# A hybrid decoder layer on one core: x is read and normalized early, the product behind the cross attention takes plain pairs first, and a simulated timeline sets the order

## The chip, the core and the metric

The kernel runs on one core of one Trainium2 chip, as one program. The metric is device time in microseconds (us) of that core from the start to the end of an execution; the times shown are medians of several executions. A core has a matmul engine (PE, with its weight loads as PEld), a vector engine (DVE), a scalar engine (ACT), a general engine (POOL) and a queue engine that issues transfers (SP). Each runs its own list of instructions in the listed order; an instruction waits until those it depends on, on whatever engine, have ended.

## The reference

One layer on 256 rows of 2048 fp32 numbers (one batch, D_FF 5632, 256 memory rows). Everything is fp32:

```
h = x
h = h + 0.5 * swiglu(rmsnorm(h, g_ffn1), w1_gate, w1_up, w1_down)     # silu(n@w_gate) * (n@w_up) @ w_down
z = rmsnorm(h, g_mix) @ w_in                                          # u, v | q | k, v
y_a = spatial_gating(u, v)        # gelu, rmsnorm of v, causal 128x128 mix of rows in 8 channel groups
y_b = window_attention_sinks(q, k, v, sinks)   # 16 heads of 64 on 2 kv heads, window 128, one sink logit a head
h = h + concat(rmsnorm(y_a), rmsnorm(y_b)) @ w_out
h = h + cross_attention(rmsnorm(h, g_x), rmsnorm(mem, g_mem), w_xq, w_xkv, w_xo)   # 4 heads of 512
h = h + 0.5 * swiglu(rmsnorm(h, g_ffn2), w2_gate, w2_up, w2_down)
out = rmsnorm(h, g_final)
```

with rmsnorm(x, g) = x * rsqrt(mean(x^2) + 1e-5) * g. The window attention is a masked softmax over 256 keys (128 in the first block) plus the sink; the cross attention is a plain softmax over the 256 memory rows.

## The kernel before

**Tiling.** The 256 rows are two blocks (TB = 2) of 128; h stays on chip for the whole program as two blocks of 128 x 2048. A product of fp32 numbers is made of three fast matmuls: each operand is split into a rounded high part and the rest as a low part, and high x high, low x high and high x low are added up in one PSUM bank. One such matmul is 128x128 by 128x512. The left operand is the activation, transposed, in *pairs* (two slices of 128 along the contraction by two row blocks, 128x4x128); the right operand is a *chunk* of weights, 128x4x512 fp32 (1 MB): two slices of the contraction by two column blocks. Multiplying a pair with a chunk is 24 matmuls (kinds N, plain, and C, with two sums) or 21 (kind S, a seven-product scheme with sums of the activation and of the weights, as in Strassen's). A *Unit* (L297) is a row of pairs and chunks that add up in the same banks, the four blocks of 256 rows by 1024 columns: products P, Q and R with numbers; names in `late` take their bank from the pool of transposes (trp, 4 banks), the others from the accumulation pool (acc, 4 banks).

**Weights.** `load` (L268 to L296) brings a chunk from HBM by SP into `raw` (3 buffers; L290 in four pieces for the first chunk, L293 for whole ones, L275 for kind S), makes the high part `wh` by a cast on ACT (L137) and the low part `wl` by a subtraction on DVE (L138), 2 buffers each; kind S adds sums on DVE and their split `t`, `th`, `tl` (1 buffer each). `push` (L341) loads a chunk and then issues the matmuls of the chunk before it (L324), so loads run one chunk ahead in the text.

**Stages.** f1 (gate/up units 0 to 10, then four down units), n2, kv, q, v, u with the spatial mix, window attention with the products mv of the memory values, mk, wo, n3, xq and the four heads of the cross attention, the product xo behind it, n4, f2 (as f1), the final norm with the stores. Names in the trace carry the stage's letters: `f1gP` is bank P of a gate/up unit of f1, `n1s` a scaled row tile of norm n1, `mvwh` the high part of an mv chunk.

**The opening.** Gate/up unit 0 (`plain_gu_unit`, L496) is plain: its pairs n0 come from xT, a transposed copy of x in HBM (L233), scaled by the gain only, and the rows are scaled by 1/rms in the silu (L451). `prep1` (L605) is called ahead of each of its 8 chunks: it loads xT for two pairs at each even chunk; at chunks 2 to 5 it loads a quarter of x (L615) and takes its squares; at chunk 6 it makes the 1/rms, and at chunks 6 and 7 it scales the rows (`n1s`, L624, on ACT), transposes them on PE (L208) and splits them into the pairs n1 of units 1 to 10, whose kinds are CCSCSCSC.

**Norms.** `next_norm` gives `on_block`, called as each 128x512 block of h is done: squares on ACT, and once the first half is done a preliminary 1/rms, by which `scaled` (L565, tile `n4s` at L568 for n4) scales the row blocks for the transposes of the pairs.

**Window attention (L744 to L809).** Two row blocks by two halves of the heads, each half in groups of scores that fill one bank: scores (`sc`, L760, PE), scaling with the mask (`scs`, L769, DVE), maximum (L773) and three small steps (to `nmx`, L778) on DVE, exponentials (L780, ACT, one for each head of the group), four transposes (`pT`, L788, PE), their copy (`pTs`, L792, DVE), and the product with v (`wop`, L796, PE). The text has it ahead of the two mv units, whose four banks are evacuated by ACT (L817) into tiles `mv` of the pool m4. The scheduler mixes both.

**Cross attention.** Per head: transposes of xq, scores, softmax (`pr`, L922), transposes of the probabilities (`xpT`, L927), product with mv, and two pairs `xo` of kind KINDS_O (NSNSNSNN). `added_unit` (L426) then multiplies them with the chunks of w_xo in two units; at the last S pair `early` adds what the sums give to h, at the last pair `late` adds the four blocks and calls `on_block`.

**The end.** `on_final` (L971) takes squares and multiplies each block of h by the final gain (`hg`, L975); the 1/rms of each row block (L116, L120, L122) then scales the eight blocks (DVE at L987, ACT at L985), and SP stores them (L988).

**What sets the order.** The text names no order between engines. A scheduler (the tile framework) takes all instructions with their dependences and buffer lifetimes and writes each engine's list: it places an instruction once it counts as ready, by priorities in the order of the text. Pool sizes (s2 7 tiles of 128x512, m4 12 tiles of 128x1024) bound how far ahead anything may be placed.

Of the kernel before, what the change touches and what calls it, by code (L numbers as in the profile page):

```python
# [14 lines left out]
P = 128  # L15
# [15 lines left out]
def layer_kernel(  # L31
# [265 lines left out]
    class Unit:  # L297


        def __init__(self, s, kinds):  # L300
            self.s = s
            self.kinds = kinds
# [6 lines left out]
            self.mixed = "S" in kinds  # L309
# [4 lines left out]
        def multiply(self, p, b):  # L314
            for name, *terms in PRODUCTS[p.kind]:
                if name not in self.banks:
                    late = ("P1", "Q6", "Q7") + (("R",) if self.mixed else ())
                    pool, tag = (trp, "tr") if name in late else (acc, "acc")
                    self.banks[name] = pool.tile([P, 512], F32, tag=tag, name=nm(self.s + name))
# [60 lines left out]
    KINDS_O = "NSNSNSNN"  # L380

# [44 lines left out]
    def added_unit(s, w, cb, pairs, on_block, kinds=KINDS_O):  # L426
        u = Unit(s, kinds)
        early, late = adds(s, 1.0, 2 * cb, on_block)
        last = len(kinds) - 1
        for i in range(len(kinds)):  # L430
            push(
                u, i, w[i, cb], lambda i=i: pairs[i],
                lambda i=i: early(u) if i == kinds.rindex("S") else late(u) if i == last else None,
# [105 lines left out]
    def next_norm(s, gcol, kinds="NNNNNNNN"):  # L539
# [25 lines left out]
        def scaled(j):  # L565
            r = [s2(s + "s") for _ in range(TB)]
            for tb in range(TB):
                nc.scalar.activation(  # L568
                    r[tb], h[:, tb, j * 512:(j + 1) * 512], AF.Copy, scale=st["est"][:, tb:tb + 1]
                )  # L570
            make(j, lambda tb, c: r[tb][:, c - j * 512:c - j * 512 + P])
# [33 lines left out]
    def prep1(i):  # L605
# [6 lines left out]
        if 2 <= i < 6:  # L612
            j = i - 2
            hj = h[:, :, j * 512:(j + 1) * 512]
            nc.sync.dma_start(hj, x[:, j * 512:(j + 1) * 512].rearrange("(b p) d -> p b d", p=P))  # L615
            for tb in range(TB):
                square_into(parts1[:, tb, j:j + 1], hj[:, tb, :], 512)
        if i == 6:
            rs1.append(rstd_of(parts1, NG, D))
        if i >= 6:  # L620
            for j in (2 * (i - 6), 2 * (i - 6) + 1):
                r = [s2("n1s") for _ in range(TB)]
                for tb in range(TB):
                    nc.scalar.activation(  # L624
                        r[tb], h[:, tb, j * 512:(j + 1) * 512], AF.Copy, scale=rs1[0][:, tb:tb + 1]
                    )
                for q in range(2):
                    n1[2 * j + q] = pair_from_rows(
                        "n1", KINDS[2 * j + q],
# [430 lines left out]
```

## Time and profile before

| what | value |
|---|---|
| median of 3 runs | 2149.03 us (2147.45 to 2151.48) |
| the profiled execution: its own time | 2150.37 us |
| its span, first to last instruction | 2147.0 us |
| mean granted clock of PE | 0.991 |
| busy: PE / PEld / DVE / ACT / POOL | 98% / 80% / 76% / 52% / 1% |
| DMA | 402.14 MB, 187 GB/s over the span |

The page gives for each engine its busy time and number of instructions; the span in 40 slices, where each digit is a tenth of busy time; and the chain of work that ended last, followed back from the end. A group's row reads: line, engine, operation, result <- operands, shapes, count, busy time and mean, idle time before it, and the work that ended that idle time. A row of the timeline is start, duration, engine, line, operation, and in brackets how long the engine idled ahead of it and what for. A busy PE is one with a matmul in its pipeline; a 128x512 matmul that takes 0.39 from start to end lets the next start after about 0.227 us (24 of a chunk follow one another in some 5.4).

### The profile page before, as it was taken

Reading aid. Unit: us, or ns where it says so; the run is one execution under the profiler, and the core shown is the slowest. Engines: PE = TensorE matmul, PEld = TensorE weight load, DVE = VectorE, ACT = ScalarE, POOL = GpSimd, SP = SyncE. Lnnn points to the kernel's source line nnn. Section 1 sums busy time; section 2 is a strip of 40 time slices with the busy share of each in tenths; the row PEclk is TensorE's granted clock in tenths of the full one; section 3 lists DMA queues with packets and bytes.
Section 4 is the critical chain, followed back from the end, with each engine's and each line's share of the span. In section 5 each row is a group of like instructions: output and inputs, shape, how many; then the busy total and the mean of one; then the engine's idle time right before and its main releaser. Section 6 shows DMA issues by size and latency. Waiting matters only on the chain.

```text
span 2147.0 us, 23708 instructions
## 1 busy us (share of the span) xinstructions
PE 2097.3 (98%) x9529; PEld 1717.3 (80%) x9529; DVE 1626.8 (76%) x1540; ACT 1114.9 (52%) x1105; POOL 17.7 (1%) x35
## 2 busy tenths in 40 slices
PE   9799999999999999999999998999999999999997
PEld 7688888888888888878877887787888888878876
DVE  5688888888787745564568666898888888887876
ACT  7555554554554555444455454665555555555443
POOL 0000000000000010000000000000000000000000
PEclk9899999999999999999999999999999999999999
DMA  7355555555555576534545543455555555555553
GB/s 295 134 199 192 199 197 196 196 196 196 196 182 210 187 242 214 177 111 147 177 163 191 192 143 116 157 196 196 198 194 201 199 208 189 195 187 196 194 202 131
DMA packets 61805, 402.14 MB, mean 187 GB/s; under 512 B 6768, under 2 KB 10880, under 8 KB 14464
## 3 DMA queue, kind: packets, MB, share of 16 engines
q1 hardware_dynamic: 60448, 396.44, 51.4%
q0 software_dynamic: 1248, 4.20, 0.7%
q8 instruction: 74, 1.21, 0.2%
q14 instruction: 35, 0.29, 0.0%
HBM read 398.52 MB, written 2.10 MB: 187 GB/s over the span
## 4 chain that ended last, share of the span: by engine, by line
PE 90%; DVE 4%; ACT 3%; issue 1%; DMA 0%; POOL 0%; SPq 0%; POOLq 0%; DVEq 0%; ACTq 0%
PE f2gQ L324 15%; PE f1gQ L324 15%; PE f1dQ L324 6%; PE f2dQ L324 6%; PE f2gP L324 5%; PE f1gP L324 5%; PE f1dP L324 3%; PE f2dP L324 3%; PE f1dR L324 2%; PE mvQ L324 2%; PE f2dR L324 2%; PE mkQ L324 2%; PE xqQ L324 2%; PE woQ L324 2%; PE mvP L324 1%
## 5 line engine op out<-in xcount | busy, mean ns | idle before, releaser
L138 DVE TENSOR_TENSOR f1gwl<-f1gw,f1gwh 128x2048 fp32r<-128x2048 f32 (+1 forms) x91 | 184.2, 2042 | 40.6 <-ACT f1gwh L137 40.5
L137 ACT CAST f1gwh<-f1gw 128x2048 fp32r<-128x2048 f32 (+1 forms) x91 | 156.0, 1715 | 91.0 <-PE f1gQ L324 66.5
L137 ACT CAST f2gwh<-f2gw 128x1536 fp32r<-128x1536 f32 (+1 forms) x88 | 153.6, 1751 | 70.2 <-PE f2gQ L324 41.5
L138 DVE TENSOR_TENSOR f2gwl<-f2gw,f2gwh 128x1536 fp32r<-128x1536 f32 (+1 forms) x88 | 182.1, 2087 | 8.5 <-ACT f2gwh L137 8.1
L137 ACT CAST f2dwh<-f2dw 128x2048 fp32r<-128x2048 f32 (+1 forms) x44 | 79.9, 1815 | 104.1 <-PE f2dQ L324 86.2
L324 PE MATMUL f2gQ<-f2gwh,n4fh 128*128 128x512 f32 x341 | 133.0, 390 | 0.0
L324 PE MATMUL f2gQ<-f2gwh,n4fl 128*128 128x512 f32 x341 | 132.9, 390 | 0.0
L324 PE MATMUL f2gQ<-f2gwl,n4fh 128*128 128x512 f32 x341 | 132.6, 390 | 0.0
L324 PE MATMUL f1gQ<-f1gwh,n1fh 128*128 128x512 f32 x330 | 130.3, 395 | 0.0
L137 ACT CAST f1dwh<-f1dw 128x2048 fp32r<-128x2048 f32 (+1 forms) x44 | 79.9, 1815 | 95.9 <-PE f1dQ L324 80.6
L324 PE MATMUL f1gQ<-f1gwh,n1fl 128*128 128x512 f32 x330 | 128.9, 391 | 0.0
L324 PE MATMUL f1gQ<-f1gwl,n1fh 128*128 128x512 f32 x330 | 128.9, 391 | 0.0
L138 DVE TENSOR_TENSOR f1dwl<-f1dw,f1dwh 128x2048 fp32r<-128x2048 f32 (+1 forms) x44 | 95.3, 2169 | 37.6 <-ACT f1dwh L137 37.4
L138 DVE TENSOR_TENSOR f2dwl<-f2dw,f2dwh 128x2048 fp32r<-128x2048 f32 (+1 forms) x44 | 95.3, 2169 | 37.3 <-ACT f2dwh L137 37.2
L138 DVE TENSOR_TENSOR f2gtl<-f2gt,f2gth 128x2048 fp32r<-128x2048 f32 x33 | 75.6, 2292 | 53.9 <-ACT f2gth L137 51.8
L137 ACT CAST f2gth<-f2gt 128x2048 fp32r<-128x2048 f32 x33 | 63.1, 1911 | 95.0 <-DVE f2gt L284 95.0
L138 DVE TENSOR_TENSOR f1gtl<-f1gt,f1gth 128x2048 fp32r<-128x2048 f32 x30 | 68.8, 2292 | 45.3 <-ACT f1gth L137 45.3
L137 ACT CAST f1gth<-f1gt 128x2048 fp32r<-128x2048 f32 x30 | 57.4, 1913 | 67.8 <-DVE f1gt L284 65.3
L324 PEld LDWEIGHTS f2gQ<-f2gwh,n4fh 128*128 128x128 f32 x341 | 64.0, 188 | 13.4
L324 PEld LDWEIGHTS f2gQ<-f2gwh,n4fl 128*128 128x128 f32 x341 | 64.0, 188 | 13.3
L324 PEld LDWEIGHTS f2gQ<-f2gwl,n4fh 128*128 128x128 f32 x341 | 64.0, 188 | 13.3
L324 PEld LDWEIGHTS f1gQ<-f1gwl,n1fh 128*128 128x128 f32 x330 | 62.3, 189 | 13.3
(616 smaller groups left out, 5823.2 us busy)
## 6 DMA issues: line engine op xcount, KB each, us to landing
f2gw<-in_w_gu SPq DMA_DIRECT2D x88, 1024.0 KB, 4.8
f1gw<-in_w_gu SPq DMA_DIRECT2D x87, 1024.0 KB, 4.9
f1dw<-in_w_down SPq DMA_DIRECT2D x44, 1024.0 KB, 4.8
f2dw<-in_w_down SPq DMA_DIRECT2D x44, 1024.0 KB, 4.8
mvw<-in_w_xkv SPq DMA_DIRECT2D x16, 1024.0 KB, 4.8
mkw<-in_w_xkv SPq DMA_DIRECT2D x16, 1024.0 KB, 4.8
wow<-in_w_out SPq DMA_DIRECT2D x16, 1024.0 KB, 4.8
xqw<-in_w_xq SPq DMA_DIRECT2D x16, 1024.0 KB, 4.8
```

The source lines that it names most:

```text
L137: nc.scalar.copy(hi, src)
L138: nc.vector.tensor_tensor(lo, src, hi.bitcast(F32), ALU.subtract)
L324: nc.tensor.matmul(self.banks[name], x, y, start=name not in self.begun, stop=self.left[name] == 0,)
```

## The change

It does four things. **prep1**: x is loaded in four quarters at chunks 1 and 2, with the squares, the 1/rms is made at chunk 3, and each of chunks 4 to 7 scales one quarter, into one tile of pool m4 (128x1024) where two tiles of s2 stood, and makes two pairs of n1. **scaled** of `next_norm` uses one m4 tile in the same way. **The cross attention's product** takes pairs of kinds KINDS_X = NNNNSNSN, two S pairs where there were three, and names the products with a bank in the pool of transposes (P1, Q5, Q6, Q7, where R was and Q5 was not). **The scheduler** is told to go by a simulated timeline, in which each instruction has an estimated duration, when it chooses what to place next on an engine.

```diff
--- before.py
+++ after.py
@@ -297,8 +297,9 @@
     class Unit:
 
 
-        def __init__(self, s, kinds):
+        def __init__(self, s, kinds, late=("P1", "Q6", "Q7", "R")):
             self.s = s
+            self.late = late if "S" in kinds else ()
             self.kinds = kinds
             self.left = {}
             for kind in kinds:
@@ -306,7 +307,6 @@
                     self.left[name] = self.left.get(name, 0) + 3 * len(terms)
             self.begun = set()
             self.banks = {}
-            self.mixed = "S" in kinds
 
         def __getitem__(self, name):
             return self.banks[name]
@@ -314,8 +314,7 @@
         def multiply(self, p, b):
             for name, *terms in PRODUCTS[p.kind]:
                 if name not in self.banks:
-                    late = ("P1", "Q6", "Q7") + (("R",) if self.mixed else ())
-                    pool, tag = (trp, "tr") if name in late else (acc, "acc")
+                    pool, tag = (trp, "tr") if name in self.late else (acc, "acc")
                     self.banks[name] = pool.tile([P, 512], F32, tag=tag, name=nm(self.s + name))
                 for an, bn in terms:
                     (ah, al), (bh, bl) = p[an], b[bn]
@@ -378,6 +377,7 @@
 
     KINDS = "CCSCSCSC"
     KINDS_O = "NSNSNSNN"
+    KINDS_X = "NNNNSNSN"
 
     KINDS_D = "NNNNSNNN" + "NSNSNSN" + "NSNNNNN"
 
@@ -423,14 +423,14 @@
 
         return early, late
 
-    def added_unit(s, w, cb, pairs, on_block, kinds=KINDS_O):
-        u = Unit(s, kinds)
-        early, late = adds(s, 1.0, 2 * cb, on_block)
+    def added_unit(s, w, cb, pairs, on_block, kinds=KINDS_O, late=("P1", "Q6", "Q7", "R")):
+        u = Unit(s, kinds, late)
+        early, end = adds(s, 1.0, 2 * cb, on_block)
         last = len(kinds) - 1
         for i in range(len(kinds)):
             push(
                 u, i, w[i, cb], lambda i=i: pairs[i],
-                lambda i=i: early(u) if i == kinds.rindex("S") else late(u) if i == last else None,
+                lambda i=i: early(u) if i == kinds.rindex("S") else end(u) if i == last else None,
             )
 
     def ffn(s, get, rs, wgu, wd, on_block, first=None):
@@ -563,12 +563,12 @@
                 scaled(j)
 
         def scaled(j):
-            r = [s2(s + "s") for _ in range(TB)]
+            r = m4(s + "s").rearrange("p (b c) -> p b c", b=TB)
             for tb in range(TB):
                 nc.scalar.activation(
-                    r[tb], h[:, tb, j * 512:(j + 1) * 512], AF.Copy, scale=st["est"][:, tb:tb + 1]
+                    r[:, tb], h[:, tb, j * 512:(j + 1) * 512], AF.Copy, scale=st["est"][:, tb:tb + 1]
                 )
-            make(j, lambda tb, c: r[tb][:, c - j * 512:c - j * 512 + P])
+            make(j, lambda tb, c: r[:, tb, c - j * 512:c - j * 512 + P])
 
         def make(j, src):
             for i in (2 * j, 2 * j + 1):
@@ -609,27 +609,27 @@
             ]
             for q in range(2):
                 n0.append(pair_from_dram("n0", xT, i + q, G_FFN1, [t[:, q] for t in quad]))
-        if 2 <= i < 6:
-            j = i - 2
-            hj = h[:, :, j * 512:(j + 1) * 512]
-            nc.sync.dma_start(hj, x[:, j * 512:(j + 1) * 512].rearrange("(b p) d -> p b d", p=P))
+        if i in (1, 2):
+            for j in (2 * i - 2, 2 * i - 1):
+                hj = h[:, :, j * 512:(j + 1) * 512]
+                nc.sync.dma_start(hj, x[:, j * 512:(j + 1) * 512].rearrange("(b p) d -> p b d", p=P))
+                for tb in range(TB):
+                    square_into(parts1[:, tb, j:j + 1], hj[:, tb, :], 512)
+        if i == 3:
+            rs1.append(rstd_of(parts1, NG, D))
+        if i >= 4:
+            j = i - 4
+            r = m4("n1s").rearrange("p (b c) -> p b c", b=TB)
             for tb in range(TB):
-                square_into(parts1[:, tb, j:j + 1], hj[:, tb, :], 512)
-        if i == 6:
-            rs1.append(rstd_of(parts1, NG, D))
-        if i >= 6:
-            for j in (2 * (i - 6), 2 * (i - 6) + 1):
-                r = [s2("n1s") for _ in range(TB)]
-                for tb in range(TB):
-                    nc.scalar.activation(
-                        r[tb], h[:, tb, j * 512:(j + 1) * 512], AF.Copy, scale=rs1[0][:, tb:tb + 1]
-                    )
-                for q in range(2):
-                    n1[2 * j + q] = pair_from_rows(
-                        "n1", KINDS[2 * j + q],
-                        lambda tb, k: r[tb][:, (2 * q + k) * P:(2 * q + k + 1) * P],
-                        G_FFN1 + 4 * j + 2 * q,
-                    )
+                nc.scalar.activation(
+                    r[:, tb], h[:, tb, j * 512:(j + 1) * 512], AF.Copy, scale=rs1[0][:, tb:tb + 1]
+                )
+            for q in range(2):
+                n1[2 * j + q] = pair_from_rows(
+                    "n1", KINDS[2 * j + q],
+                    lambda tb, k: r[:, tb, (2 * q + k) * P:(2 * q + k + 1) * P],
+                    G_FFN1 + 4 * j + 2 * q,
+                )
 
     n2, on2, rs2_ = next_norm("n2", G_MIX)
     ffn(
@@ -941,7 +941,7 @@
                           for b in range(2) for m, p in ((vh, ph), (vh, pl), (vl, ph))]
                 products(pv[:, i, :], passes)
             i = 2 * hd + half
-            kind = KINDS_O[i]
+            kind = KINDS_X[i]
             xo.append(Pair("xo", kind))
             if kind == "N":
                 split(xo[i].base[0].rearrange("p k t -> p (k t)"),
@@ -956,7 +956,7 @@
 
     n4, on4, rs4_ = next_norm("n4", G_FFN2, KINDS)
     for cb in range(2):
-        added_unit("xo", w_xo, cb, xo, on4)
+        added_unit("xo", w_xo, cb, xo, on4, KINDS_X, ("P1", "Q5", "Q6", "Q7"))
     flush()
 
 
@@ -1053,7 +1053,7 @@
         for k, v in arrays.items()
     ]
     args.append(nc.dram_tensor("out", (T, D), F32, kind="ExternalOutput").ap())
-    with tile.TileContext(nc) as tc:
+    with tile.TileContext(nc, schedule_with_timeline_sim=True) as tc:
         layer_kernel(tc, *args)
     r = run_bass_kernel_spmd(nc, [arrays], core_ids=[0])
     return r.results[0]["out"].reshape(1, T, D)
```

The changed file is a line shorter from L310 on: its L323 is L324 of before, and so on.

The lists change in nearly every stage. Three places follow. First SP's list, from the first transfer of weights on (`f1gw`; `n0r` are pieces of xT, `h` quarters of x, numbers count tiles). Before:

```order
L290 DMA f1gw_129<-in_w_gu 128x512 x4
L293 DMA f1gw_144<-in_w_gu 128x2048
L233 DMA n0r_180<-in_xT 128x2x256
L233 DMA n0r_186<-in_xT 128x2x256
L615 DMA h<-in_x 128x2x512
L293 DMA f1gw_197<-in_w_gu 128x2048
L615 DMA h<-in_x 128x2x512
L293 DMA f1gw_232<-in_w_gu 128x2048
L233 DMA n0r_264<-in_xT 128x2x256
L233 DMA n0r_270<-in_xT 128x2x256
```

With the change:

```order
L290 DMA f1gw_129<-in_w_gu 128x512 x4
L615 DMA h<-in_x 128x2x512 x2
L293 DMA f1gw_154<-in_w_gu 128x2048
L615 DMA h<-in_x 128x2x512 x2
L293 DMA f1gw_212<-in_w_gu 128x2048
L293 DMA f1gw_248<-in_w_gu 128x2048
L233 DMA n0r_190<-in_xT 128x2x256
L233 DMA n0r_196<-in_xT 128x2x256
L233 DMA n0r_280<-in_xT 128x2x256
L233 DMA n0r_286<-in_xT 128x2x256
```

The four quarters of x stand in pairs around the second chunk, and the xT pieces of chunks 2 and 4 behind the fourth.

Next PE's list in the window attention, from the last matmuls of mv's first unit (`mvQ`) to the first of its second (`mvP`). Before:

```order
L324 MATMUL mvQ_1179_6706<-mvwh_6864,mTfh_6275 128x512
L788 MATMUL pT_6551<-ident,scs_6541 128x128 x2
L760 MATMUL sc_6569<-kT_5383,qT_5661 128x256
L788 MATMUL pT_6551<-ident,scs_6541 128x128 x2
L760 MATMUL sc_6569<-kT_5383,qT_5661 128x256
L324 MATMUL mvQ_1179_6706<-mvwh_6864,mTfl_6276 128x512
L324 MATMUL mvQ_1179_6706<-mvwl_6865,mTfh_6275 128x512
L796 MATMUL wop_6463<-vv_5376,pTs_6556 128x64
L796 MATMUL wop_6463<-vv_5381,pTs_6556 128x64
```

Two more products `wop` follow, then `mvP` of the second unit. With the change, its first rows:

```order
L323 MATMUL mvQ_1175_6702<-mvwl_6861,mTfh_6271 128x512
L796 MATMUL wop_6396<-vv_5372,pTs_6421 128x64 x4
L760 MATMUL sc_6427<-kT_5379,qT_5657 128x128 x4
L788 MATMUL pT_6444<-ident,scs_6432 128x128
L760 MATMUL sc_6462<-kT_5379,qT_5636 128x256 x2
L788 MATMUL pT_6444<-ident,scs_6432 128x128 x3
L796 MATMUL wop_6396<-vv_5372,pTs_6449 128x64 x4
L788 MATMUL pT_6475<-ident,scs_6465 128x128 x4
L796 MATMUL wop_6459<-vv_5372,pTs_6480 128x64
L796 MATMUL wop_6459<-vv_5377,pTs_6480 128x64
```

Between the first unit's last matmul and the second's first there are 62 attention instructions now, and no other; before, each group of the attention had matmuls of mv beside it up to here.

On ACT, the evacuation of the first bank of mv's first unit (L817) stands, before:

```order
L780 ACTIVATE scs_6436,den_6401<-scs_6436,nmx_6442 128x128 x4
L137 CAST mvwh_6834<-mvw_6833 128x2048
L780 ACTIVATE scs_6469,den_6464<-scs_6469,nmx_6475 128x256 x2
L137 CAST mvwh_6864<-mvw_6863 128x2048
L780 ACTIVATE scs_6493,den_6464<-scs_6493,nmx_6499 128x256 x2
L137 CAST mvwh_6922<-mvw_6921 128x2048
L780 ACTIVATE scs_6517,den_6464<-scs_6517,nmx_6523 128x256 x2
L802 ACTIVATE esk_6465<-esk_6465 128x8
L780 ACTIVATE scs_6541,den_6464<-scs_6541,nmx_6547 128x256 x2
L137 CAST mvwh_6928<-mvw_6927 128x2048
L817 ACTIVATE mv_6669<-mvP_1176_6685,rs_6333 128x512
```

and with the change:

```order
L780 ACTIVATE scs_6404,den_6397<-scs_6404,nmx_6410 128x128 x4
L137 CAST mvwh_6918<-mvw_6917 128x2048
L137 CAST mvwh_6924<-mvw_6923 128x2048
L802 ACTIVATE esk_6398<-esk_6398 128x8
L780 ACTIVATE scs_6432,den_6397<-scs_6432,nmx_6438 128x128 x4
L780 ACTIVATE scs_6465,den_6460<-scs_6465,nmx_6471 128x256 x2
L780 ACTIVATE scs_6489,den_6460<-scs_6489,nmx_6495 128x256 x2
L780 ACTIVATE scs_6513,den_6460<-scs_6513,nmx_6519 128x256 x2
L802 ACTIVATE esk_6461<-esk_6461 128x8
L780 ACTIVATE scs_6537,den_6460<-scs_6537,nmx_6543 128x256 x2
L780 ACTIVATE scs_6568,den_6563<-scs_6568,nmx_6574 128x256 x2
L817 ACTIVATE mv_6665<-mvP_1172_6681,rs_6329 128x512
```

The casts of mv's weights stood between the exponentials and now stand ahead of them; in both lists the evacuation stands behind the exponentials shown.

Last DVE's list at the end of the program, from the addition of the first block of the last down unit to the first scaled output. Before:

```order
L391 SCALAR_TENSOR_TENSOR h<-f2dP_2578_14849,h 128x512
L975 TENSOR_TENSOR hg_15067<-h,gf_10228 128x512
L391 SCALAR_TENSOR_TENSOR h<-f2dQ_2579_14856,h 128x512
L975 TENSOR_TENSOR hg_15072<-h,gf_10228 128x512
L391 SCALAR_TENSOR_TENSOR h<-f2dR_14863,h 128x512
L116 TENSOR_REDUCE ss_15084<-partsf_10230 128x1
L120 TENSOR_SCALAR ms_15086<-ss_15084 128x1
L987 TENSOR_SCALAR hg_14818<-hg_14818,rs_15088 128x512
```

With the change:

```order
L391 SCALAR_TENSOR_TENSOR h<-f2dP_2560_14818,h 128x512
L975 TENSOR_TENSOR hg_15036<-h,gf_10197 128x512
L391 SCALAR_TENSOR_TENSOR h<-f2dQ_2561_14825,h 128x512
L391 SCALAR_TENSOR_TENSOR h<-f2dR_14832,h 128x512
L975 TENSOR_TENSOR hg_15041<-h,gf_10197 128x512
L391 SCALAR_TENSOR_TENSOR h<-f2dQ_2563_14839,h 128x512
L116 TENSOR_REDUCE ss_15053<-partsf_10199 128x1
L975 TENSOR_TENSOR hg_15046<-h,gf_10197 128x512
L120 TENSOR_SCALAR ms_15055<-ss_15053 128x1
L987 TENSOR_SCALAR hg_14787<-hg_14787,rs_15057 128x512
```

The first scaled block stood behind three additions and two products with the gain; it stands now behind four and three.

In all, PE has 9432 instructions where it had 9426, DVE 1530 where it had 1542, ACT 1000 where it had 1007; those of SP and POOL that move data are as many as before.

## Prediction

> **What bounds the kernel now.** I read the page's busy shares and its chain of waits first, then busy time by stage, then what the matmul engine (PE) waited for. The page:
>
> ```profile
> PE 2097.3 (98%) x9529; PEld 1717.3 (80%) x9529; DVE 1626.8 (76%) x1540; ACT 1114.9 (52%) x1105; POOL 17.7 (1%) x35
> ...
> PE 90%; DVE 4%; ACT 3%; issue 1%; DMA 0%; POOL 0%; SPq 0%; POOLq 0%; DVEq 0%; ACTq 0%
> ```
>
> PE is busy for 2097.3 of 2147.0 us and carries 90% of the chain. An order of instructions can win only the 49.7 us in which PE is idle and what it loses at a lower clock, and it can lose as much as it likes. Where those microseconds lie, by stage (span; busy us of PE, PEld, DVE, ACT, POOL; granted clock; DMA share; GB/s):
>
> ```profile
> 54.00:107.00 53.00, 40.37 (x171) 32.43 (x170) 36.50 (x41) 29.01 (x37) 0.00 (x0) 0.84 0.36 133
> 107.00:805.00 698.00, 695.82 (x3166) 574.73 (x3165) 557.76 (x482) 362.05 (x304) 7.24 (x12) 1.00 0.55 199
> 912.00:966.00 54.00, 52.45 (x252) 39.95 (x252) 32.47 (x55) 22.66 (x48) 0.00 (x0) 0.97 0.32 113
> 1288.00:1342.00 54.00, 46.22 (x242) 38.90 (x241) 32.50 (x42) 24.05 (x37) 1.12 (x2) 0.94 0.32 116
> 1342.00:1396.00 54.00, 50.31 (x219) 40.04 (x217) 44.56 (x47) 34.24 (x42) 0.71 (x1) 0.97 0.43 156
> 1396.00:2093.00 697.00, 694.79 (x3088) 567.66 (x3089) 591.71 (x515) 368.21 (x291) 0.69 (x1) 1.00 0.55 197
> 2093.00:2147.00 54.00, 42.11 (x186) 34.53 (x184) 35.40 (x42) 21.66 (x28) 1.10 (x2) 0.93 0.37 132
> ```
>
> The two long feed-forward stretches idle 2.2 us each in some 700: nothing is to be had there. Four places hold nearly all: the end of gate/up unit 0 (12.6 us idle), the window attention (1.55), the cross attention with its product (7.8 and 3.7), the tail (11.9). What PE waited for there (us in total, times, longest):
>
> ```profile
> PE n L208 <- ACT n1s L624: 9.1, 3, 5.2
> PE xpT L927 <- DVE pr L922: 4.5, 2, 2.8
> PE f1gP L324 <- ACT f1sg L451: 3.6, 1, 3.6
> PE n L208 <- ACT n4s L568: 2.5, 1, 2.5
> ...
> PE mvP L324 <- ACT mv L817: 1.6, 1, 1.6
> ```
>
> **The opening: a gain.** Early x means that the 32 transposes of n1, with their scaling and splits, move from the end of unit 0 to chunks 2 to 6 of it, under its matmuls. Rows for the prices:
>
> ```profile
> 9.00:12.00 3.00, 3.00 (x8) 2.34 (x7) 1.17 (x2) 0.72 (x2) 0.00 (x0) 1.00 0.99 387
> ...
> 11.90 1.90 ACT L137 CAST f1gwh<-f1gw 128x2048 fp32r<-128x2048 f32 x1 [1.95 <-DMA f1gw<-in_w_gu]
> 13.71 1.70 ACT L131 ACTIVATE n0h<-n0r,sm 128x256 fp32r<-128x256 f32 x4
> ...
> 52.18 2.29 DVE L138 TENSOR_TENSOR f1gwl<-f1gw,f1gwh 128x2048 fp32r<-128x2048 f32 x1 [2.05 <-ACT f1gwh L137]
> ...
> 69.79 1.28 ACT L451 ACT_TABLE_LOAD   x1
> 71.08 0.69 ACT L451 ACTIVATE f1sg<-f1gP,rs 128x512 f32<-128x512 f32 x1
> ...
> 71.82 0.79 PE L324 MATMUL f1gP<-f1gwh,n1fh 128*128 128x512 f32 x1 [3.57 <-ACT f1sg L451]
> ...
> 86.62 0.39 PE L324 MATMUL f1gP<-f1gwh,n1fh 128*128 128x512 f32 x1
> ```
>
> First what it costs. One megabyte of x now stands ahead of weight chunk 1, at 387 GB/s 2.7 us, so its cast starts at 14.6 and not at 11.90 and ends at 16.5, when chunk 0 has been done for 0.8 us; its low part comes 0.4 late. Chunk 2 needs xT's second pieces, which SP now issues behind chunks 2 and 3, and on ACT the cast of chunk 3, on DVE its low part, stand ahead of their splits. Chunk 1 ends at about 22.3 and frees the buffer; cast 1.9 and one split 0.42 make 24.65 (a wait of 2.35), the low part 2.2 makes 26.85 (1.3 more). These 4.85 us are lost ahead of chunk 3. From there nothing waits by my walk: five chunks of 24 matmuls at 0.227 and 32 transposes at about 0.115 end unit 0 at 62.4. Unit 1 still needs bank P, emptied by the first silu: after the last cast (59.3), seven n1 pieces (3.2), the table load (1.28) and the silu (0.69) it is 64.5, and the cast of its second chunk ends at 66.4. 42 matmuls and 8 transposes later, unit 1's chunk 2 starts at 76.9, where the row has 86.62: 9.7 less. The clock may fall in the 2 us wait; half of a 1.6 us price leaves **8.9** (5 with waits that I missed; 17 if none of the waits occur and unit 1 starts at once).
>
> **Steady units, down products, n2, kv, q, v, u, mk, wo: nothing.** The new order sends eight matmuls of the next chunk's high part before its low part. I walked one f1 unit and the starts and ends of the stages: casts (1.9) and low parts (2.2) are ready before PE asks, as the two rows with 2.2 us idle say of before. At the start of f2 I find about **1.0** more waiting (cast of its second chunk behind the last xo chunk). The price if this cover is gone is a rival.
>
> **Window attention: a loss, the largest term.** Rows of one group of heads in before (score, mask and maximum on DVE, two exponentials on ACT, transposes, copy, product):
>
> ```profile
> 951.70 0.69 DVE L792 COPY pTs<-pT 128x512 f32<-128x512 f32 x1
> 952.32 0.69 DVE L769 SCALAR_TENSOR_TENSOR scs<-sc,band 128x512 f32<-128x512 f32 x1
> 953.05 0.69 DVE L773 TENSOR_REDUCE mx<-scs 128x2 f32<-128x512 f32 x1
> ...
> 954.04 0.16 DVE L778 TENSOR_SCALAR nmx<-mx 128x2 f32<-128x2 f32 x1
> ...
> 954.30 0.51 ACT L780 ACTIVATE scs<-scs,nmx 128x256 f32<-128x256 f32 x1
> 954.81 0.49 ACT L780 ACTIVATE scs<-scs,nmx 128x256 f32<-128x256 f32 x1
> ...
> 939.33 1.13 PE L760 MATMUL sc<-kT,qT 64*128 64x256 f32 x4
> ...
> 951.22 0.44 PE L788 MATMUL pT<-ident,scs 128*128 128x128 f32 x2
> ...
> 958.74 1.00 PE L796 MATMUL wop<-vv,pTs 128*128 128x64 f32 x8
> ...
> 960.55 0.68 ACT L817 ACTIVATE mv<-mvP,rs 128x512 f32<-128x512 f32 x1
> ...
> 962.00:964.00 2.00, 2.00 (x7) 1.56 (x6) 1.56 (x4) 1.28 (x3) 0.00 (x0) 0.52 0.00 0
> ...
> 1324.00:1328.00 4.00, 3.05 (x24) 2.64 (x22) 3.75 (x7) 3.28 (x9) 0.00 (x0) 1.00 0.00 0
> ```
>
> In before, matmuls of mv's first unit stand between the groups and hide each chain; when they run out, mv's second unit waits 1.6 us for the evacuation of its bank (960.55). In the new order the first unit is spent five groups earlier. Behind its last matmul stand 62 attention instructions in a row, and ACT lists the evacuation of bank P behind the exponentials of those groups, which wait for one another: group by group through PE, DVE, ACT and PE again. From the last mv matmul (call it 0): product 1.0 and scores 1.16 end at 2.2; mask 0.62; the low part of the next weights 2.2, which waits in between; maximum and three small steps 1.15; four exponentials 1.55; the next scores (1.13) pass between the transposes; copy: the next group's mask starts at 9.0. One group behind it takes 6.4 (its scores come after the product: copy 0.7, product 1.0, scores 1.1, mask to the last small step 1.9, exponentials 1.0, transposes 0.6). Three take 5.05 each: copy 0.62, mask to exponentials 1.92, 0.51 for the first exponential, transposes, scores 1.13, transposes 0.44, with gaps under 0.2. The sixth mask starts at 30.6, its exponentials end at 33.5, bank P is free at 34.3. PE's own work in that time is six products (6.0), scores 6.8, transposes 4.2: 17.0. So it idles **17.3**. Behind the first gap (4.5 us) the clock may be halved for some 3.4 us, 1.6 lost. Against that before's 1.55 and the half clock behind it (0.52 in the row, about 1.6) are saved: net **15.7** lost. From below: 4.1 a group, where the scores never stand in the way, and no lower clock, 9.5; from above, half the clock throughout, up to 25. I take the walk, whose durations are all rows of the same instructions.
>
> The Trainium skill ("TensorE: Matmul & The Clock Gate", What's actually happening) says that the clock is halved after an idle window of about 3.4 us. By it only the first gap would cost anything, the same sum; the row at 962 shows 0.52 after a wait of 1.6 us, and the row at 1324 full clock with a quarter idle, so the measurement leaves both open.
>
> **Cross attention and its product: a gain.** Rows for two prices:
>
> ```profile
> 1371.40 1.23 DVE L280 TENSOR_TENSOR xot<-xow 128x1024 f32<-128x1024 f32 x1
> ...
> 1376.09 1.47 ACT L137 CAST xowh<-xow 128x1536 fp32r<-128x1536 f32 x1
> ```
>
> Before loses 7.78 + 3.69 idle and, by the clocks 0.94 and 0.97, 2.8 + 1.5: 15.8. With four plain pairs first, 46 and 27 xo matmuls (10.4 and 6.1 us) stand between the scores and the transposes of heads 2 and 3, and 34 (7.7) ahead of n4's transposes, so the waits of 4.5 and 2.5 go. What remains by my walk: 1.1 for a split of 128x1024 on DVE, 2.3 where the cast of 128x1536 and its low part stand ahead of a head's split, 1.9 for a whole cast whose buffer is freed by the matmul just before, 1.5 in small ones; one S pair fewer per unit is 2 x 3 matmuls, 1.36; one fall of the clock 1.6. 15.8 - 9.8 = **6.0** gained (2 to 11).
>
> **Tail: a loss.**
>
> ```profile
> 2130.65 0.39 PE L324 MATMUL f2dP<-f2dwl,f2afh 128*128 128x512 f32 x1
> ...
> 2134.73 0.39 PE L324 MATMUL f2dQ<-f2dwl,f2afh 128*128 128x512 f32 x1
> ...
> 2131.07 0.69 DVE L391 SCALAR_TENSOR_TENSOR h<-f2dP,h 128x512 f32<-128x512 f32 x1 [2.79 <-PE f2dP L324]
> ...
> 2135.50 0.49 DVE L987 TENSOR_SCALAR hg<-hg,rs 128x512 f32<-128x512 f32 x1 [0.73 <-POOL rs L122]
> ```
>
> Block P now ends 12 matmuls before the last (2.72) and not 18 (4.08), and the first rstd stands behind all four additions and three products of DVE. Its scaling starts 3.2 after the last matmul, not 0.77, and the stores, which the last square waits for, follow: **2.4** lost (1 to 3).
>
> **The sum**, against the profiled run (span 2147.0, its time 2150.4): -8.9 + 1.0 + 15.7 - 6.0 + 2.4 = +4.2, so 2154.6 there. That run lies 1.3 above the median 2149.0 of the runs shown, so I say **2154**. About 0.2%, or 4.3 us, is what a measurement can tell from no change.
>
> **Rivals.** *The stretch costs its lower bound:* 9.5 and not 15.7, 2148 to 2150, the same. For it: the copies and masks are pipelined in the rows; against it: the scores stand between the transposes in the listed order. *The fills work fully:* the opening's 4.85 and half of the cross attention's waits do not occur, as the pieces of x land among the weights; with a stretch near its bound 2142, faster. For it: DMA at 387 GB/s still has room after 33 us; against it: ACT and DVE lists put the splits behind the casts whatever the DMA does. *The steady units pay:* the low parts, listed behind eight high matmuls, arrive late where DVE is busiest; decisive from 0.3 us a unit, and at 0.5 in each of 20 units 10 us, 2164, slower. For it: DVE is busy for 592 of 697 us in f2; against it: my walk. Half clock all along the stretch ends there too. *The change does less than it says* (engines hold to an order only as far as their waits force them): no row shows an engine overtaking its own list.
>
> **How the numbers follow.** Forecast 0.45 (2149 to 2160, a third of it within 0.2%), lower bound 0.2, full fills 0.2, steady units or clock 0.15. Slower: two thirds of 0.45 and 0.15, 0.45; same 0.15 and 0.2, 0.35; faster 0.20. The range 2141 to 2166 takes in the full fills and most of the steady case.
>
> **What would show it.** Right: PE idle for 15 us or more between two mv units, waiting for mv's evacuation and for copies of pT; unit 1 at 62 to 66 us; no wait of PE for n4s; the first scaled hg 3 us behind the last matmul. Wrong: window attention with under 10 us idle, idle time over 5 us in either feed-forward stretch, or unit 1's chunk 2 later than 80 us.

## The result and the profile after

The changed kernel takes 2171.5 us (median, 2170.4 to 2173.1) beside 2148.6 of the kernel before on the same chip: a ratio of 1.0105, 95% interval 1.0088 to 1.0123, 23 us slower. The forecast was 2154 with a range of 2141 to 2166. The sign of the likeliest case was right; the size was not, and the time lies outside the range.

The profiled execution is 2170.4 us with a span of 2168.4, 21.4 more than before's span. The page after, its busy times and the chain of waits:

```profile
PE 2101.5 (97%) x9535; PEld 1726.0 (80%) x9535; DVE 1613.2 (74%) x1528; ACT 1109.7 (51%) x1098; POOL 19.3 (1%) x35
...
PE 56%; DVE 7%; DMA 2%; ACT 2%; issue 1%; DVEq 0%; POOLq 0%; POOL 0%; ACTq 0%
```

PE is busy 4.2 us more for six matmuls more (1.4 us), and idle 17.2 us more. Busy time that grows by more than the added work points to a lower clock. To see where, I took from both traces the start of the last matmul of each stage and compared the lengths of the stages. The table has the change and the first five experiments of the next section, in us against before, each from one profiled execution (e3 and e4 show -1.2 in a stage that their edits do not touch, so about 1 us there tells nothing):

```
stage (ends with its last matmul)   change   e1     e2     e3     e4     e5
f1 gate/up (with the opening)        -7.0   -6.8   -6.9   -6.5   -1.3   -8.0
f1 down                              +2.4   +3.0   -0.1   -0.1   -0.1   +3.1
kv, q, v                             -1.2   -1.2    0.0    0.0    0.0   -1.2
u, attention and mv, mk             +21.9  +20.7    0.0   -1.2   -1.2   -6.3
wo                                   +3.7   +3.1    0.0    0.0    0.0   +2.9
xq, cross attention, xo              -6.7  +12.9  -15.0   +0.5  -15.0  -10.0
f2 gate/up                           +2.4   +6.0   +1.7   +0.1   +1.7   +2.7
f2 down                              +3.8   +2.1    0.0    0.0   -0.1   +2.8
tail                                 +2.2   +2.2    0.0    0.0    0.0   +2.2
span                                +21.4  +41.9  -20.3   -7.2  -15.9  -12.0
```

(e1 the simulated timeline alone, e2 the edits without it, e3 early x alone, e4 pair kinds and larger tiles alone, e5 the change with the attention spread out.)

The answering rows by stage of the kernel after, with the columns of the rows by stage in the prediction (span, busy of the five engines, clock, DMA share, GB/s):

```profile
9.00:63.00 54.00, 50.28 (x219) 40.30 (x218) 33.59 (x50) 43.75 (x77) 0.72 (x1) 0.97 0.68 258
...
916.00:1033.00 117.00, 103.78 (x443) 80.16 (x441) 53.19 (x82) 36.30 (x70) 0.00 (x0) 0.81 0.27 98
1033.00:1123.00 90.00, 90.00 (x413) 74.80 (x412) 47.72 (x38) 41.82 (x37) 0.00 (x0) 1.00 0.53 186
1123.00:1223.00 100.00, 92.38 (x416) 74.10 (x415) 80.99 (x85) 52.19 (x61) 1.12 (x1) 0.98 0.47 168
```

One row stands out: from 916 to 1033 PE idles 13.2 us, and the granted clock is 0.81. What PE waited for over the whole span (us in total, times, longest):

```profile
PE pT L788 <- ACT scs L780: 9.3, 6, 4.6
PE wop L796 <- DVE pTs L792: 3.9, 5, 0.8
PE xoP L323 <- ACT xowh L137: 3.8, 2, 2.0
PE woR L323 <- DVE n3fl L132: 3.2, 1, 3.2
...
PE f2dP L323 <- DVE f2dwl L138: 2.5, 5, 0.9
PE f2gP L323 <- DVE h L391: 2.3, 1, 2.3
PE f1gP L323 <- ACT n0h L131: 2.2, 1, 2.2
PE f1dR L323 <- DVE n2fl L132: 1.7, 1, 1.7
```

The first two are the chain of the window attention, as forecast; n1s, n4s and pr, which headed the list before, are gone from it. Of the others, the forecast had the wait for n0h (the opening) and one of the two for xowh. The rest are mostly at places where one unit hands its banks to the next, and the forecast had nothing there. Now the attention itself, PE's timeline from the last product on (start, duration, in brackets the idle time ahead and what ended it):

```profile
934.82 1.00 PE L796 MATMUL wop<-vv,pTs 128*128 128x64 f32 x8
935.75 1.16 PE L760 MATMUL sc<-kT,qT 64*128 64x128 f32 x8
941.50 0.48 PE L788 MATMUL pT<-ident,scs 128*128 128x128 f32 x1 [4.60 <-ACT scs L780]
941.91 2.07 PE L760 MATMUL sc<-kT,qT 64*128 64x256 f32 x4
943.91 0.90 PE L788 MATMUL pT<-ident,scs 128*128 128x128 f32 x3
945.60 1.97 PE L796 MATMUL wop<-vv,pTs 128*128 128x64 f32 x8 [0.78 <-DVE pTs L792]
948.02 1.18 PE L788 MATMUL pT<-ident,scs 128*128 128x128 f32 x4 [0.45 <-ACT scs L780]
949.98 1.97 PE L796 MATMUL wop<-vv,pTs 128*128 128x64 f32 x8 [0.78 <-DVE pTs L792]
951.88 2.07 PE L760 MATMUL sc<-kT,qT 64*128 64x256 f32 x4
956.62 0.69 PE L788 MATMUL pT<-ident,scs 128*128 128x128 f32 x2 [2.67 <-ACT scs L780]
...
976.39 1.18 PE L788 MATMUL pT<-ident,scs 128*128 128x128 f32 x4 [0.54 <-ACT scs L780]
977.46 0.80 PE L323 MATMUL mvP<-mvwh,mTfh 128*128 128x512 f32 x1
...
982.31 0.49 PE L323 MATMUL mvP<-mvwl,mTfh 128*128 128x512 f32 x1
```

Before the wait of 4.60 a product takes 1.00; behind it 1.97, and scores take 2.07 where they took 1.13 in the kernel before. That doubling goes on for the whole row, and twelve matmuls into the next unit. The granted clock of the row, and of those twelve:

```profile
934.82:977.46 42.64, 29.42 (x102) 20.15 (x100) 17.99 (x42) 9.87 (x33) 0.00 (x0) 0.54 0.13 48
977.46:982.30 4.84, 4.84 (x12) 3.84 (x12) 0.69 (x1) 1.67 (x3) 0.00 (x0) 0.50 0.01 3
```

### The profile page after: what moved, and what is told of

Read it like the earlier page. It is cut to its first block, busy times and chain, and to the rows that moved or that the text cites. A ratio compares the mean times of both kernels' runs of the same rounds, so it can differ in the third digit from the quotient of the medians.

```text
span 2168.4 us, 23703 instructions
## 1 busy us (share of the span) xinstructions
PE 2101.5 (97%) x9535; PEld 1726.0 (80%) x9535; DVE 1613.2 (74%) x1528; ACT 1109.7 (51%) x1098; POOL 19.3 (1%) x35
## 4 chain that ended last, share of the span: by engine, by line
PE 56%; DVE 7%; DMA 2%; ACT 2%; issue 1%; DVEq 0%; POOLq 0%; POOL 0%; ACTq 0%
PE f2gQ L323 14%; PE f2gP L323 5%; PE f2dQ L323 4%; PE f2dP L323 2%; PE mvQ L323 2%; PE xqQ L323 2%; PE mkQ L323 2%; PE f2dR L323 2%; PE xoQ L323 2%; PE mvP L323 1%; PE woQ L323 1%; PE mvR L323 1%; PE xqR L323 1%; PE vQ L323 1%; PE uQ L323 1%
## 5 line engine op out<-in xcount | busy, mean ns | idle before, releaser
L323 PE MATMUL f2gQ<-f2gwh,n4fl 128*128 128x512 f32 x341 | 132.6, 390 | 0.0
L323 PE MATMUL f2gQ<-f2gwh,n4fh 128*128 128x512 f32 x341 | 132.5, 389 | 0.0
L323 PE MATMUL f1gQ<-f1gwh,n1fh 128*128 128x512 f32 x330 | 128.7, 390 | 0.0
L323 PE MATMUL f1gQ<-f1gwh,n1fl 128*128 128x512 f32 x330 | 128.4, 389 | 0.0
L323 PE MATMUL f2gQ<-f2gwl,n4fh 128*128 128x512 f32 x341 | 120.0, 389 | 0.0
L323 PE MATMUL f1gQ<-f1gwl,n1fh 128*128 128x512 f32 x330 | 116.0, 390 | 0.0
L323 PEld LDWEIGHTS f2gQ<-f2gwh,n4fh 128*128 128x128 f32 x341 | 64.0, 188 | 13.5
L323 PEld LDWEIGHTS f2gQ<-f2gwh,n4fl 128*128 128x128 f32 x341 | 64.0, 188 | 13.4 <-DVE n4fl L138 0.2
L323 PEld LDWEIGHTS f2gQ<-f2gwl,n4fh 128*128 128x128 f32 x341 | 64.0, 188 | 13.2
L323 PE MATMUL f2gP<-f2gwh,n4fh 128*128 128x512 f32 x176 | 69.6, 396 | 3.1 <-DVE h L391 2.3
```

The source lines that it names most:

```text
L323: nc.tensor.matmul(self.banks[name], x, y, start=name not in self.begun, stop=self.left[name] == 0,)
```

## The experiments

Theory after seeing the result: the new lists, which the simulated timeline writes, make the loss, most of it in the attention row, where waits and half clock go together; the edits themselves gain. Rivals: the edits lose by themselves or only gain under the new lists; the attention's chain has to be paid somewhere in any order; the clock is incidental.

**e1 to e4: taking the change apart.** The timeline alone,

```diff
-    with tile.TileContext(nc) as tc:
+    with tile.TileContext(nc, schedule_with_timeline_sim=True) as tc:
```

on the kernel before (e1); the change without that line (e2); the kernel before with the new `prep1` only (e3); the change without that line and with the old `prep1` (e4).

> The kernel before with the simulated timeline as the only edit. If the new lists make the loss (theory): the row of attention instructions between the two mv units appears here too at half clock (some 40 us from the last matmul of one unit to the first of the other), the waits at the ends of down units, wo and f2 as well, and the edits' gains are missing: 2174 to 2186 us. If the edits and the lists only lose together (rival): 2149 to 2160.

> All edits of the change but the simulated timeline. Theory: opening 7 to 9 gained, cross attention 3 to 6 gained, nothing else moves: 2134 to 2141 us. Rival (the edits need the new order, or lose by themselves): 2147 or more.

> Only the early x of the first unit, in the order of before. Theory: unit 1's third chunk starts 7 to 9 us earlier and nothing else moves: 2139 to 2143 us. Rival (the plain order leaves the scaled rows behind the casts, so the wait only moves): 2146 to 2150.

> Only the pair kinds behind the cross attention and the larger tiles of the norms, in the order of before. Theory: the waits for the probabilities of heads 2 and 3 (4.5 us) and for n4 (2.5) go, two S pairs fewer cost 1.4: 2142 to 2146 us. Rival (the plain order puts other work there and nothing goes): 2148 to 2151.

Against before (2148.2): e1 2188.2 us, ratio 1.0184 (1.0168 to 1.0199); e2 2129.3, 0.9911 (0.9894 to 0.9927); e3 2142.9, 0.9975 (0.9964 to 0.9986); e4 2134.2, 0.9932 (0.9917 to 0.9946). So the edits gain 19 us, of which early x has 5 and the kinds and tiles 14, and these add up. The timeline costs 40 us on the kernel before and 42 on the edited one (2171.5 less 2129.3). The rival that the edits lose, or need the new order, falls. e3's time came as expected (its third chunk of unit 1 starts 6.5 earlier, a little under the 7 to 9); the others went beyond the bounds. e1 lost more, as its cross attention with the old kinds takes 12.9 longer. e4, and with it e2, gained more: 15.0 in the cross attention, nearly all of the 15.8 that the prediction counts as lost there before, where I had expected only the two longest waits to go. Both pay 1.7 of it back in f2's gate/up stage.

The row of e1 that answers to the attention row above, from the last product ahead of the wait to the first matmul of the second mv unit:

```profile
935.60:978.40 42.80, 29.59 (x103) 20.27 (x101) 17.99 (x42) 9.98 (x33) 0.00 (x0) 0.55 0.13 47
```

It is the same row in length and clock, without any of the edits. In e2 the longest waits of PE (us in total, times, longest) are

```profile
PE f1gP L323 <- ACT f1sg L451: 5.1, 1, 5.1
PE f1gP L323 <- ACT f1gwh L137: 3.2, 2, 2.2
PE woP L323 <- ACT wowh L137: 2.1, 3, 1.1
PE xoP L323 <- DVE h L391: 1.6, 1, 1.6
```

where neither n4s nor pr is named, which before stood among the four longest.

**e5: the attention spread out under the timeline.** The attention's text becomes a generator that ends a group at each `yield`, and the mv units call one group ahead of each chunk:

```diff
+    def attention():
...
+                    yield
...
+    groups = attention()
     mv = [m4("mv") for _ in range(4)]
     for cb in range(2):
-        pv_ = unit("mv", w_xkv, 2 + cb, mT)
+        u = Unit("mv", "N" * 8)
+        for i, p in enumerate(mT):
+            next(groups, None)
+            push(u, i, w_xkv[i, 2 + cb], lambda p=p: p)
+        flush()
```

> The change with one thing more: the text of the window attention is cut into its twelve groups, and one group stands ahead of each chunk of the mv products, so that the simulated timeline has matmuls of mv beside every group. Theory (the 42.6 us between the mv units is the schedule's loss, waits and half clock together): the whole stage falls back to before, 22 us less, 2147 to 2152 us, no window at half clock there. Rival (the attention chain must be paid for somewhere, and evacuations only wait elsewhere): 2160 or more.

2140.5 us, ratio 0.9965 (0.9952 to 0.9978): 31 us under the change, and faster than before, more than the theory had asked. The profiled spans lie 33.4 apart, of which 28.2 are in the stages u to mk (21.9 + 6.3 in the table) and 3.3 in the cross attention (see e10). From 900 to 990 PE has no break, and full clock:

```profile
900.00:930.00 30.00, 30.00 (x149) 24.70 (x149) 15.44 (x21) 12.23 (x22) 0.00 (x0) 1.00 0.48 168
930.00:960.00 30.00, 30.00 (x145) 24.34 (x144) 17.07 (x21) 13.54 (x22) 0.00 (x0) 1.00 0.41 148
960.00:990.00 30.00, 30.00 (x145) 24.24 (x144) 16.19 (x22) 10.77 (x17) 0.00 (x0) 1.00 0.44 149
```

All that PE waits for from 880 to 1100 is

```profile
PE wop L798 <- DVE pTs L794: 0.8, 1, 0.8
```

The rival falls: the chain of dependent pieces is hidden, not moved. The twelve groups do not all end beside mv: its last matmul starts at 990.8, the attention's last product at 1041.5, so the last groups run beside matmuls of mk.

**e6: useless work in the breaks.** Twelve matmuls on the identity ahead of each group's transposes in the second row block, into the bank that these overwrite:

```diff
+FILL = 12
...
                 pt = bank("pT")
+                if n == 1:
+                    for _ in range(FILL):
+                        nc.tensor.matmul(pt[:, :P], ident, ident, start=True, stop=True)
```

> The change with twelve useless 128x128 fp32 matmuls on the identity in each of the eight groups of the second row block, into the bank that the group's transposes then write. Five groups of the row between the mv units have them, 60 matmuls, 6.9 us at full clock and 13.8 at half. Theory (the clock stays at half because PE is never busy long enough without a break): the added work fills the breaks, the granted clock in the row comes back to 1.0, its products take 1.0 us and not 1.97, and the row takes less than the 42.6 us, 34 to 40, though PE has more to do. Rival (the chain through DVE and ACT sets the pace and the clock follows something else): clock 0.5 all along, row of 48 us or more.

2176.7 us, ratio 1.0138 (1.0121 to 1.0155): 5 us over the change. Neither expectation holds as written. The row takes 43.5 us (936.58 to 980.11), not 34 to 40 and not 48. One of my numbers was wrong: twelve such matmuls take 2.9 us at full clock and not 1.4, as the second row here shows (a matmul is two entries of it), so that the five groups have 14.7 us more work, and not 6.9. On the clock it decides, though. Rows of PE's timeline, then the granted clock from the first transposes on, in three pieces:

```profile
958.20 4.60 PE L788 MATMUL pT<-ident 128*128 128x128 f32 x24
...
975.03 2.94 PE L788 MATMUL pT<-ident 128*128 128x128 f32 x24
...
979.19 1.10 PE L800 MATMUL wop<-vv,pTs 128*128 128x64 f32 x8 [0.78 <-DVE pTs L796]
```

```profile
943.26:951.05 7.79, 7.79 (x40) 6.51 (x40) 2.18 (x5) 1.10 (x6) 0.00 (x0) 0.69 0.28 119
954.55:962.72 8.17, 8.17 (x36) 7.10 (x36) 1.78 (x5) 1.09 (x4) 0.00 (x0) 0.58 0.00 0
962.72:980.11 17.39, 16.05 (x122) 14.31 (x121) 6.75 (x17) 4.65 (x13) 0.00 (x0) 1.00 0.00 1
```

In both of the first pieces PE works without a break for some 8 us, and within them the clock comes back (if it is either half or full, the means of 0.69 and 0.58 put that some 4.8 and 6.9 us in, an estimate); between them it has breaks of 1.79 and 0.78 and falls again. In the last, three groups run at full clock with two breaks, 0.56 and 0.78, some 6 us apart. Breaks of that size stand in the change's row at half clock, but in pairs: from 956.62 to 977.46 PE idles 3.9 of 20.8 us there, and 1.3 of 17.4 here. So single breaks of that size do not lower the clock, and the fillers that close most of them bring it back. Whether the size of the breaks or their number kept it at half in the change is not separated. Fourteen us of added work made the row 0.9 us longer.

**e7 and e11: banks at the hand-over of units.** The waits woR (3.2) and f1dR (1.7) are for the low part of n3 and n2, whose transposes use the pool of banks in which R lies. Q5 takes R's place there, as in the xo units, in wo (e7) or in the down units (e11):

```diff
-        added_unit("wo", w_out, cb, ny, on3)
+        added_unit("wo", w_out, cb, ny, on3, KINDS_O, ("P1", "Q5", "Q6", "Q7"))
```

```diff
-            u = Unit(s + "d", kinds)
+            u = Unit(s + "d", kinds, ("P1", "Q5", "Q6", "Q7"))
```

> The change with the names of late products of the wo units as in the xo units (Q5 and not R in a bank of the pool of transposes). Theory (the 3.2 us wait of woR for a split of n3 is a wait for a bank of that pool, in which the new order has put transposes ahead of woR): it goes, wo takes 2 to 4 us less, 2167 to 2170 us. Rival (the split is late in DVE's list whatever the bank): the wait moves to the next reader, 2171 to 2174.

> The change with Q5 in place of R among the names with a bank in the pool of transposes, in the down units of f1 and f2. Theory (two causes there: a wait for a bank of that pool, 1.7 us in f1, and low parts that stand behind additions on DVE, up to 0.94 each): the first goes, the second stays; f1's down units 1 to 2.5 us less, f2's the same, 2169 to 2171. Rival (bank names are the whole cause): both go back, 2165 to 2167.

e7 2165.6 us, ratio 1.0089 (1.0074 to 1.0104); e11 2166.8, 1.0087 (1.0071 to 1.0104). These intervals overlap with the change's, so the times alone do not tell them from it; the stages do. Both times lie below the theory's range, and e11's in that of its rival, so the stages have to decide between these two as well. In e7 wo costs 0.7 more than before and not 3.7, and the wait of woR is gone:

```profile
PE woP L323 <- DVE wowl L138: 2.4, 2, 1.8
PE n L208 <- DVE h L391: 1.3, 1, 1.3
```

In e11 f1's down units are at -0.1 and not +2.4, while f2's lose no less, +5.1 beside +3.8. So the bank is the cause in wo and f1 and not in f2, as the theory had it. Most of the rest of both gains is in the cross attention, at -9.6 and -10.0, which neither edit touches (see e10).

**e8: kinds without the larger tiles**, in the order of before:

> Order of before, late x, small tiles in the norms: only the pair kinds and bank names behind the cross attention. Theory (the plain pairs, which let xo matmuls stand between scores and transposes, make the gain): 2134 to 2138 us, as with the larger tiles. Rival (the larger tile of n4, which has a pool of its own, makes half of it): 2140 to 2144, with a wait for n4s of 2 us or more.

2134.2 us, ratio 0.9940 (0.9925 to 0.9955), the same as e4. The kinds make the gain; the larger tiles of the norms are worth nothing that shows in that order.

**e10: late x under the timeline.** The change with `prep1` as it was.

> The change with x read and normalized as before (late), everything else as in the change. Theory, new since the runs before (the simulated timeline alone already gains what the opening has to give): 2170 to 2173 us, the same as the change. Rival (the early x makes the 7 us in the change as it does in the plain order): 2177 to 2180.

2164.3 us, ratio 1.0076 (1.0061 to 1.0091): under the change, and not the same as it. The opening is 1.6 shorter than with early x (-8.6 in place of -7.0): under the new lists early x gains nothing in the opening and costs its waits there. Another 3.3 are again in the cross attention, over 1300 us after the edit. There ACT's list differs by the place of one cast. In the change, ACT waits 1.83 for the sums of an S chunk and only then casts the next chunk (first fence); in e10 that cast stands ahead of the same wait (second):

```profile
1398.74 2.57 ACT L568 ACTIVATE n4s<-h,rs 128x512 f32<-128x512 f32 x4 [1.19 <-POOL rs L122]
1403.14 1.91 ACT L137 CAST xoth<-xot 128x2048 fp32r<-128x2048 f32 x1 [1.83 <-DVE xot L284]
1404.95 1.89 ACT L137 CAST xowh<-xow 128x2048 fp32r<-128x2048 f32 x1
```

```profile
1397.07 2.57 ACT L568 ACTIVATE n4s<-h,rs 128x512 f32<-128x512 f32 x4 [1.20 <-POOL rs L122]
1399.70 1.91 ACT L137 CAST xowh<-xow 128x2048 fp32r<-128x2048 f32 x1
1401.56 1.91 ACT L137 CAST xoth<-xot 128x2048 fp32r<-128x2048 f32 x1
```

PE waits 2.00 for that cast in the change:

```profile
1406.89 0.50 PE L323 MATMUL xoP<-xowh,xofh 128*128 128x512 f32 x1 [2.00 <-ACT xowh L137]
```

and 0.62 for the low part behind it; neither wait is in e10, nor in e5, e6, e7 and e11. The lists under the timeline change far from an edit, so some 3 us of the change's loss are a matter of a cast that fell on the wrong side of a wait, and as much of the gains of e5, e7, e10 and e11 is no merit of their edits.

**e9: the edits with the attention spread out, without the timeline.**

> The three edits without the simulated timeline, with one attention group ahead of each chunk of mv. Theory (spreading by itself gains what the stage still idles and loses at a lower clock, 1.6 of waits and some 2 of clock): 2124 to 2128 us, a little under the edits alone. Rival (the groups' evacuations come between the casts in the order by priorities and nothing is won): 2128 to 2134.

2125.6 us, ratio 0.9895 (0.9880 to 0.9910), as the theory had it and the fastest of all. The wait of mvP for its bank is gone and the stage is 3.7 shorter in the profile than before's; by the times alone, e9 and e2 overlap.

## Why the prediction was right and wrong

**The opening** was forecast at -8.9. Unit 1's third chunk, behind 48 matmuls of the unit, starts at 78.1 where before had 86.6: -8.6. (The stage in the table has -7.0, as 1.5 are lost again at its end, see the steady units.) The walk held step by step: the waits of unit 0 are 0.21, 0.21, 2.17 and 1.12, where I had 0.8, 0.4, 2.35 and 1.3; unit 1 starts at 65.5 and not 64.5; its third chunk at 78.1 and not 76.9. The clock fell once, as the 0.97 of the first row above shows: 1.6 over its 54 us, where I had half of that. What the forecast said of the cause was wrong: e1 gains 6.8 in the stage without early x. The wait for n1s (9.1 in before) is in none of the change, e1, e3 and e10. The gain is the end of unit 0 being filled, which either the edit or the new lists bring about, and together they bring it once.

**The window attention** was forecast at +15.7 and is +21.9 with its neighbours u and mk. Of the single stages this one missed by most. The mechanism was right: the same 62 instructions, the evacuation behind the exponentials of the groups, one group after the other. The step that failed is the price of the clock: I had 1.6 us of lower clock behind the first gap and full clock from there. The row shows half clock all along. PE's own work grew from the 17.0 us that I had to 29.4, and ate some of the waits, which came to 13.2 and not 17.3: 42.6 us and not 34.3. Behind the row twelve matmuls stand some 0.43 apart and not 0.227, 2.4 us more. Less the 1.6 that I had counted, row and matmuls come to 9.1 above the walk and the stage to 6.2: the rest of the stage gave 2.9 back, which I had not forecast. My upper bound ("half the clock throughout, up to 25") was the case that came; I gave it a place in a rival of 0.15.

I had read the Trainium skill ("TensorE: Matmul & The Clock Gate", What's actually happening) by half. It says that an idle window lowers the clock, and also that some 3.4 us of sustained work bring it back, with windows that run freely. The trace agrees with the second half: in the row no piece without a break is longer than 4.0 us (949.98 to 953.95) and the clock stays at half; behind it, it takes 5.9 us without a break (976.39 to 982.3), in e1 3.8 (977.25 to 981.04, where the matmuls go from 0.43 to 0.227 apart), and in e6 under 8. The first half agrees less: before's clock fell to 0.52 after a wait of 1.6, in the change it fell some 1.2 us into the wait of 4.60 (the mean is 0.63 from 936.91 to 941.50), and f2's start kept 1.00 after a wait of 2.3.

**"Steady units, down products, n2, kv, q, v, u, mk, wo: nothing"** is the second step that failed, and in the sum the larger: +1.5 at the end of f1's gate/up units, +2.4 in f1's down units, +3.7 in wo, +3.8 in f2's down units, -1.2 ahead of v, 10.2 in all. I had walked one gate/up unit and carried it over to units of other kinds. Within, the gate/up units did hold: from 100 us on f1's has no wait but 2.1 us in its last 12, where before has 0.6. The losses are where units hand over: R's bank (e7, e11), additions to h, and in f2's down units low parts that come up to 0.94 late behind additions and sums on DVE. The late low parts are the mechanism of my rival of the steady units, at other places and half its price (waits of 5.3 us at the end of f1's gate/up units and in the down units). For f2's down units it is read from the trace and was not tested.

**The start of f2** was forecast at +1.0 and is +2.4: a wait of 2.3 for an addition that empties a bank, where I had a wait for a cast.

**Cross attention and its product** came out at -6.7 for -6.0, with the remaining waits that I had listed (a cast whose buffer is freed by the matmul just before: 1.9 forecast, 1.76 found, and 2.00 for another cast, the one of e10). But it is not what the edit is worth: that is 15.0 in the plain order, and 19.6 under the timeline (12.9 + 6.7), where the old kinds would have lost. That the number came so near is in part luck: the stage's waits are 8.3 us where I had 6.8, and the fall of the clock that I had put at 1.6 did not come (1.00 from 1223 to 1439).

**The tail** was forecast at +2.4 and is +2.2, the first scaled block 3.0 us behind the last matmul (3.2 forecast).

The sum missed by 17.2: 6.2 in the attention, 10.2 in steady units, 0.3 in the opening, 1.4 at f2's start, less 0.9 in the rest. Two of my cases, half clock along the row and losses in steady units, came together. I had set them beside each other as ways to the same 2164, some 10 above the forecast, though nothing kept both from coming; with both it would have been about 2174, and 2171.5 was measured. One reading of before was also too strong: the four places that I named hold 37.6 of its 49.7 us of idle time, which is three quarters and not nearly all.

## What to carry to other kernels

A gap that PE spends waiting can be priced twice: once for the wait, and once for all the work behind it until PE has run for several us without a break (3.8 to 6.9 here); a row of short dependent pieces did not get there in 41 us. When several changes come together, walk each under the order that it will run in, and price the order by itself: here the edits gained 19 us and the order lost 42. Independent work belongs beside the dependent chain and not ahead of it: spreading the attention's groups over the chunks of mv and mk was worth 28 us.

## What the runs showed of the hardware that I had not expected

The clock that fell within a wait of 4.60 us stayed at half for 41 us behind it, under a PE that was busy 69% of the row (29.42 of 42.64), and 14.7 us of useless matmuls in its breaks made the row only 0.9 us longer. Single breaks of 0.56 and 0.78 us, the size of those that stood in the row at half clock, did not lower it once it was full.
